# The end of an RWKV-7 layer: other buffers for the raw token sums, the last third of those sums made in two steps, and weight splits placed behind the last root

## The chip, the cores and the metric

The kernel runs on one core of a Trainium2 chip. The metric is the device time of one launch in microseconds (us), as the median of several runs; lower is better. Engines are named as in the profile: PE is TensorE, DVE is VectorE, ACT is ScalarE, POOL is GpSimd, and SP is the engine whose queue issues most of the DMAs. POOL's queue issues the DMAs that add to what lies in memory.

## The reference

Two residual layers work on x of 512 tokens by 2048 columns, all in float32. Layer 0 is gated differential attention; the change does not touch it. Layer 1 is gated RWKV-7 time mixing:

```
p = h @ w_in                                   # h = rms_norm(x)
p = p + (token_shift(p) - p) * mu
r, k, v, g, dw, da = split(p)
...
y = wkv7_scan(r, decay, k, v, -kk, kk * a)     # a 64x64 state per head, 32 heads
mean = y.mean(-1);  var = square(y - mean).mean(-1)
y = (y - mean) * rsqrt(var + GN_EPS)           # per head and token
y = y * gn_w + gn_b + sum(r * k * r_k) * v
y = y * silu(g)
x = x + y @ w_out                              # w_out is 2048 x 2048
```

## The kernel before

**Products.** A float32 product is made as three passes on operands split into a rounded high part and the rest (`mm3`, L116 to L122; L119 is the matmul). A block of weights that a DMA has brought (`wraw`, or the tiles `T2`, `TT0` and `TT1`, which the profile prints as T and TT) is split in halves by `split_w` (L88): ACT casts the high part `wh` (L110), DVE subtracts to get the low part `wl` (L111). There are four buffers of each, and a half block feeds six matmuls in turn: `wh` first, `wl` one matmul later.

**The scan.** The 32 heads are worked on as 16 pairs, j = 0 to 15, in chunks of 64 tokens. `scan_pair` (L1890 to L1934) carries one pair's state through eight chunks. Each chunk is a ring over three engines: a matmul (L1898), two ACT copies `rhs` (L1901), a matmul (L1911), two ACT copies `VS` (L1913), a matmul (L1920), two DVE steps that make the next `VS` (L1924), and two POOL copies `SA` (L1906). Between these steps the scheduler puts matmuls of other products. Each operation of a step stands in the fixed order of its engine, so anything that waits ahead of an ACT copy holds up the ring. After the last chunk come the outputs Y (L1944, L1948), the centring `yc` on DVE (L1952 to L1961), and `normal` (L1964): the squares `ysq` on ACT (L1969), their sums `var` on DVE (L1971), and then the reciprocal root by `rsqrt` (L57 to L70), eleven small DVE operations of which the last writes `rsg`. `scale` (L1977) multiplies `yc` by it, and `finish_y` (L1983) transposes the result on PE (L1989). For pair 15 this is the last root of the kernel, and the gated rows that follow are the last two rows of y that the output product needs.

**The output product.** `y @ w_out` is made for two halves of the columns (`one` and `two`) by a scheme with seven products of blocks in place of eight. It needs sums of blocks of weights (`wsums`) and sums of blocks of tokens. `Sums` (L934) makes both in device memory: a copy is a DMA of SP's queue (L954), an addition is an accumulating DMA of POOL's queue (L958). Of the token sums there are four, S1 to S4, in three thirds i = 0, 1, 2; each is 256 KB. With y's row blocks a, b, c and d they are S1 = b + d, S2 = S1 + a, S4 = S2 + c and S3 = a + b. Each call of `step` does the next item of a list. `Forms.load` (L911) brings the thirds of a sum into raw buffers `fraw` by SP's queue (L916), in a ring of six; `Forms.make` splits them: ACT writes the high part (L931) and DVE the low part (L933), both named fS. DVE's part is ordered behind a given instruction; ACT's is placed where the scheduler finds room.

**The order.** `outputs_of` (L1114 to L1160) is the written order of the end: the blocks "12" of both halves, those "11" of `one` and then of `two`, in whose middle `finish(None)` ends the last scan, and then `rest` of both halves. `pace` feeds split rows of y and takes a step of `Sums`. The scheduler may start instructions of later lines earlier where their operands allow it; `issue_after` gives it an order of two instructions and no more. Each engine then works through its own list strictly in order.

**Buffers.** The six raw buffers of `Forms` are two in the tile LT, two in BK and two of four in G1 (L2109 to L2111). `ysq` lives in LT as well, so the LT pair is free only after the last `ysq`.

Of the kernel before, what the change touches and what calls it, by code (L numbers as in the profile page):

```python
# [13 lines left out]
F32 = mybir.dt.float32  # L14
# [4 lines left out]
ALU = mybir.AluOpType  # L19
# [4 lines left out]
P = 128  # L24
# [33 lines left out]
def rsqrt(g, out, v, n, tag):  # L58

    nc = g.nc  # L60
    sh = g.small.tile([P, n], I32, name="rs_i", tag=tag + "i")
    t = g.small.tile([P, n], F32, name="rs_t", tag=tag + "t")
    nc.vector.tensor_single_scalar(sh[:], v.bitcast(I32), 1, ALU.logical_shift_right)
    nc.vector.tensor_scalar(sh[:], sh[:], -1.0, float(0x5F3759DF), ALU.mult, ALU.add)
    y = sh[:].bitcast(F32)
    for i in range(3):
        nc.vector.tensor_mul(t[:], y, y)
        nc.vector.scalar_tensor_tensor(t[:], t[:], -0.5, v, ALU.mult, ALU.mult)
        o = out if i == 2 else y
        nc.vector.scalar_tensor_tensor(o, t[:], 1.5, y, ALU.add, ALU.mult)  # L70


def load_w(g, raw, block, k0, ks, queue=None):
# [18 lines left out]
@urgent  # L92
def split_w(g, block, kg, cols, k0, raw=None):


    nc = g.nc
    held = raw is not None and block is not None
    if raw is None:
        raw = g.wraw.tile([P, kg, cols], F32, name="wraw", tag="wraw")
        load_w(g, raw, block, k0, slice(0, kg))  # L100
    n = kg // 2
    his, los = [], []
    for k in range(0, kg, n):
        hi = g.wh.tile([P, n, cols], F32R, name="wh", tag="wh")
        lo = g.wl.tile([P, n, cols], F32R, name="wl", tag="wl")
        with ExitStack() as after:
            if held and k0 + k < 4:
                for ins in g.made[k0 + k - 1] if k0 + k else [g.made_prm]:
                    after.enter_context(g.tc.issue_after(ins))
            nc.scalar.copy(hi[:], raw[:, k : k + n])  # L110
            g.split = nc.vector.tensor_sub(lo[:], raw[:, k : k + n], hi[:].bitcast(F32)).ins  # L111
        his.append(hi)
        los.append(lo)
    return Halves(his, n), Halves(los, n)
# [369 lines left out]
class Feed:  # L484
# [8 lines left out]
    def load(self, upto):  # L493
        for k in range(len(self.raw), min(upto, self.n)):
            self.raw.append(self.home(k))
            self.g.nc.sync.dma_start(out=self.raw[k], in_=self.src[k * P : (k + 1) * P, :])
# [257 lines left out]
NS = 6  # L754
KG = 2
# [147 lines left out]
class Forms:  # L903
# [4 lines left out]
        self.at = {nm: [None] * len(homes) for nm in FORMS}  # L908
        self.raw = {}

    def load(self, nm):  # L911
        self.raw[nm] = []
        for i in range(len(self.homes)):
            self.ring.append(self.ring.pop(0))
            raw = self.ring[-1]
            self.g.nc.sync.dma_start(out=raw, in_=self.src[FORMS.index(nm), i])  # L916
            self.raw[nm].append(raw)
# [22 lines left out]
class Sums:  # L940
# [27 lines left out]
    def token_sums(self, i):  # L968
        (a, b), (c, d) = [[self.yd[(FIRST[kb] + i * KG) * P : (FIRST[kb] + (i + 1) * KG) * P,
                                   256 * t : 256 * t + 256].rearrange("(k p) t -> p k t", p=P) for t in range(2)]  # L970
                          for kb in range(2)]
        s1, s2, s3, s4 = [self.forms[n, i] for n in range(4)]
        return [lambda: (self.copy(s1, b), self.copy(s3, a)), lambda: (self.add(s1, d), self.add(s3, b)),
                lambda: self.copy(s2, s1), lambda: self.add(s2, a), lambda: self.copy(s4, s2),
                lambda: self.add(s4, c)]
# [140 lines left out]
def outputs_of(g, one, two, feed, finish, more):  # L1116


    def pace(n):
        feed(4 + n // 2, g.m)  # L1120
        g.wsums.step()

    def then(nm):
        forms.make(nm)
        if nm in order:
            forms.load(order[nm])

    forms, order = one.sums, {"S2": "S4", "S4": "S3"}
    N, s = NS // KG, 0
    for i in range(N + 1):  # L1130
        for b in (one, two):
            pace(s)
            if i == N - 1 and b is two:
                b.want("11")
            b.first12(i)
            s += KG
    two.take("11", two.y)
    for i in range(N):
        pace(s)
        pace(s + 1)  # L1140
        one.first11(i)
        s += KG
        if not i:
            more(0)
            one.want("11")
            one.take("11", one.y)
    one.take("11", one.X, ALU.subtract)
    forms.load("S1")
    for i in range(N):
        two.first11(i)  # L1150
        if i == 0:
            forms.load("S2")
        if i == 1:
            finish(None)
            more(1)
    two.take("11", two.X, ALU.subtract)
    forms.make("S1", g.m.ins)
    one.rest(then, finish)
    two.rest()

# [325 lines left out]
NG = 4  # L1486
# [73 lines left out]


class Pair:
    done, now, scale = False, False, None


def mus(g, i, j):
# [397 lines left out]
def normal(g, p):  # L1964

    nc, w, yc = g.nc, g.work, p.yc
    NG = 2 * NT
    sq = g.low.tile([P, NG, C], F32, name="ysq", tag="LT", bufs=1)
    nc.scalar.activation(sq[:], yc[:], AF.Square)  # L1969
    var = g.small.tile([P, NG], F32, name="var", tag="var")  # L1970
    nc.vector.reduce_sum(var[:], sq[:], AX.X)  # L1971
    nc.vector.tensor_scalar(var[:], var[:], 1.0 / C, GN_EPS, ALU.mult, ALU.add)
    rs = g.small.tile([P, NG], F32, name="rsg", tag="rsg")
    rsqrt(g, rs[:], var[:], NG, "r8")

    def scale():
        nc.vector.tensor_mul(yc[:], yc[:], rs[:, :, None].to_broadcast([P, NG, C]))  # L1977

    p.scale = scale
    if p.now:  # L1980
        p.scale()
# [12 lines left out]
def layer1(g, aps):  # L1994
    nc, tc = g.nc, g.tc
    with ExitStack() as cx:
# [38 lines left out]
        for j in range(D // P):  # L2035
            p = pairs[j]
            if j:
                others = [(1, lambda p=p: turn_keys(g, p, 0)), (2, lambda p=p: turn_keys(g, p, 4)),
                          (4, lambda p=p: turn_values(g, p))]
                if j > 1:  # L2040
                    others.append((5 if j + 1 < D // P else 3, lambda i=j - 2: finish_y(g, i, pairs[i])))
                gaps = (6, 7) if j == 1 else (7, 8) if j < D // P - 1 else (5, 6)
                chain(g, j - 1, pairs[j - 1], 3 if j > 1 else 22, *gaps, others)
            ar = stage2(g, j, r, p)
            for q in pairs[j - 2 : j - 1] if j > 1 else ():
                q.now = True
                if q.scale:
                    with tc.issue_after(ar.ins):
                        q.scale()
            p.now = j + 2 >= D // P  # L2050

            def behind(m, j=j, p=p):
                if j > 1:
                    pairs[j - 2].chain.finish(g)
                with tc.issue_after(m.ins):
                    gram(g, j, p)
                p.solve = Solve(g, t_solve(g, j, p))
            hooks = [(12 if 0 < j < LAG else 18, behind)]
            if j + 1 == D // P:
                hooks.append((39, lambda m, p=p: [mask_gram(g, p, h, m) for h in range(2)]))  # L2060
            stage_v(g, j, p, proj(2, j, behind=hooks + kept()))
            turns = ()
            if j == 0:
                turns = ((9, lambda m: turn_keys(g, p, 0)), (15, lambda m: turn_keys(g, p, 4)),
                         (27, lambda m: turn_values(g, p)))
            if j + 1 < D // P:
                begin(j + 1, turns or kept())

            def finished(m, i=j - LAG):
                with tc.issue_after(m.ins):  # L2070
                    gated(g, i, pairs[i], held)
                g.ys.extend((held, pairs[i].y))

            if j:
                gps = proj(3, j - 1, behind=[(36, finished)] * (j >= LAG) + kept())
                held = gate(g, j - 1, gps, None)
            if j + 1 < D // P:
                r = receptances(j + 1)
        chain(g, j, p, 3, 4, 5, whole=True)
        gts = [held, gate(g, j, proj(3, j), "E")]  # L2080
        feed = Feed(g, g.yd2, KT - 2, lambda k: w.tile([P, T], F32, name="yr", bufs=1, tag=(
# [24 lines left out]
                 {"S1": one("VS"), "S2": one("VS"), "S4": one("xH", "xL"), "S3": one("y", "y")},  # L2106
                 {"S1": one("th0", "th1"), "S2": one("r", "k"), "S4": one("E", "thg"), "S3": one("yc", "v")})

        raws = [g.low.tile([P, 2, KG, 256], F32, name="fraw", tag=t, bufs=1)[:, i] for t in ("LT", "BK") for i in range(2)]  # L2109
        both = w.tile([P, 4, KG, 256], F32, name="fraw", tag="G1", bufs=2)  # L2110
        raws += [both[:, i] for i in range(4)]  # L2111
        sums = Forms(g, g.wsums.forms, raws, homes)

        def sides(c0, early):
# [37 lines left out]
def body(ctx, tc, nc, aps):  # L2152
    g = Ctx()
    g.nc, g.tc = nc, tc
    g.last, g.first, g.ticks, g.kept, g.stored = None, [], 0, None, 0
    g.chains, g.later, g.soon, g.late, g.state, g.solve = [], [], [], [], None, None
    g.hp = ctx.enter_context(tc.tile_pool(name="hp", bufs=16))
    g.wh = ctx.enter_context(tc.tile_pool(name="whp", bufs=4))
# [48 lines left out]
```

## Time and profile before

| what | value |
|---|---|
| median of 3 runs | 2069.09 us (2068.36 to 2069.86) |
| the profiled execution's own time | 2067.63 us |
| its span, first to last instruction | 2065.9 us |
| mean granted TensorE clock | 0.999 |
| DVE, ACT, POOL busy | 82%, 62%, 21% |

A line of the timeline gives the start of a group of instructions in us of the span, its length, the engine, the line of the kernel, the operation, what it writes and reads (buffer numbers left out) with its shape, the number of instructions, and in brackets the idle time of the engine just before it with the instruction or DMA that ended it. Matmuls overlap, so the pace of PE is read from the distance between starts and not from the lengths. A window's line gives the busy time of each engine in that stretch, the number of its instructions, the granted clock (1.00 is full), the DMA engines' busy share and the GB/s moved. A line of DMA issues gives the KB of one and the us from issue to landing.

### The profile page before, as it was taken

What the parts mean: (1) busy time and instruction counts of PE and PEld (TensorE: products, weight loads), DVE (VectorE), ACT (ScalarE), POOL (GpSimd) and SP (SyncE); (2) the same over time, 40 slices, a digit from 0 to 9 for tenths busy, and PEclk for the clock granted to TensorE, in tenths of its full rate; (3) what the DMA queues carried; (4) which work ended last, traced back from release to release, by engine and by line L of the source; (5) the groups of instructions that cost most, each with busy time, mean ns of one, the idle gap of its engine ahead of it and who ended that gap; (6) DMA issues with size and microseconds to landing.
All of it is one profiled execution on the core that took longest, in us unless ns stands there. A gap on an engine that the chain in (4) does not pass through costs nothing.

```text
span 2065.9 us, 35395 instructions
## 1 busy us (share of the span) xinstructions
PE 2044.4 (99%) x11888; PEld 1682.6 (81%) x11888; DVE 1690.7 (82%) x4417; ACT 1288.6 (62%) x3065; POOL 433.4 (21%) x751
## 2 busy tenths in 40 slices
PE   9999999999999999999999999999999999999999
PEld 8888878888888878888778888888888888876787
DVE  5979788897888976576888888888888898887865
ACT  5667676676767754455666666666666666666543
POOL 0020211202111000101232332233333232342000
PEclk9999999999999999999999999999999999999999
DMA  6387877869778665832234443434445332347663
GB/s 201 115 172 184 163 173 175 177 173 168 176 166 212 182 204 180 201 104 95 96 104 131 131 120 97 127 111 130 110 126 136 99 96 86 108 134 214 204 229 133
DMA packets 113943, 306.95 MB, mean 149 GB/s; under 512 B 13920, under 2 KB 35056, under 8 KB 113472
## 3 DMA queue, kind: packets, MB, share of 16 engines
q1 hardware_dynamic: 71056, 204.15, 30.5%
q0 software_dynamic: 28272, 84.52, 23.3%
q10 hardware_dynamic: 14432, 16.01, 2.2%
q8 instruction: 94, 1.54, 0.3%
q14 instruction: 89, 0.73, 0.1%
HBM read 288.63 MB, written 47.45 MB: 163 GB/s over the span
## 4 chain that ended last, share of the span: by engine, by line
PE 43%; DVE 3%; DMA 2%; ACT 1%; issue 1%; SPq 0%; DVEq 0%; ACTq 0%
PE pp L119 31%; PE pt L119 4%; PE sm L1898 1%; PE gp L1669 1%; PE sm L1920 1%; PE sm L1911 1%; DMA forms<-yd 1%; PE Y L1944 1%; DVE wl L111 1%; PE pt L1729 1%; PE px L1796 0%; PE Y L1948 0%; PE px L1811 0%; DMA yr<-yd 0%; PE pt L1989 0%
## 5 line engine op out<-in xcount | busy, mean ns | idle before, releaser
L119 PE MATMUL pp<-hH,wh 128*128 128x512 f32 x1024 | 416.9, 407 | 0.0
L119 PE MATMUL pp<-hL,wh 128*128 128x512 f32 x1024 | 412.1, 402 | 0.0
L119 PE MATMUL pp<-hH,wl 128*128 128x512 f32 x1024 | 411.9, 402 | 0.0
L110 ACT CAST wh<-wraw 128x512 fp32r<-128x512 f32 (+1 forms) x412 | 254.1, 618 | 211.0 <-PE pp L119 139.7
L111 DVE TENSOR_TENSOR wl<-wraw,wh 128x512 fp32r<-128x512 f32 (+1 forms) x412 | 289.9, 705 | 78.2 <-ACT wh L110 73.6
L119 PE MATMUL pp<-wh,hH 128*128 128x512 f32 x784 | 311.7, 398 | 0.7 <-DVE G L383 0.4
L119 PE MATMUL pp<-wl,hH 128*128 128x512 f32 x784 | 308.5, 393 | 0.0
L119 PE MATMUL pp<-wh,hL 128*128 128x512 f32 x784 | 307.8, 393 | 0.0
L119 PEld LDWEIGHTS pp<-hH,wh 128*128 128x128 f32 x1024 | 192.9, 188 | 38.0 <-issue 1.8
L119 PEld LDWEIGHTS pp<-hH,wl 128*128 128x128 f32 x1024 | 193.2, 189 | 33.2
L119 PEld LDWEIGHTS pp<-hL,wh 128*128 128x128 f32 x1024 | 193.2, 189 | 31.3
L119 PE MATMUL pp<-wh,S 128*128 128x512 f32 x672 | 214.4, 394 | 0.0
L616 ACT CAST wh<-T 128x512 fp32r<-128x512 f32 x224 | 137.2, 620 | 91.5 <-PE pp L119 70.9
L1906 POOL COPY SA<-VS 64x64 f32<-64x64 f32 x224 | 76.1, 340 | 494.6 <-DVE VS L1924 446.2
L119 PEld LDWEIGHTS pp<-wh,hH 128*128 128x128 f32 x784 | 147.7, 188 | 31.0 <-DVE acc L1056 0.7
L119 PEld LDWEIGHTS pp<-wh,hL 128*128 128x128 f32 x784 | 148.0, 189 | 30.0
L119 PEld LDWEIGHTS pp<-wl,hH 128*128 128x128 f32 x784 | 147.8, 188 | 28.7 <-DVE wl L111 0.3
L617 DVE TENSOR_TENSOR wl<-T,wh 128x512 fp32r<-128x512 f32 x224 | 150.6, 685 | 23.3 <-ACT wh L616 22.6
L589 POOL DMA_DIRECT2D T<-in_da_w_in_dram x84 | 72.2, 860 | 385.6 <-DMA wraw<-in_da_w_in_dram 193.9
L1762 DVE SCALAR_TENSOR_TENSOR tmpl<-LT,n,Tm 128x60 f32<-128x60 f32 (+24 forms) x496 | 135.9, 274 | 13.3
L119 PEld LDWEIGHTS pp<-wh,S 128*128 128x128 f32 x672 | 124.8, 188 | 24.5
L119 PE MATMUL pp<-wl,S 128*128 128x512 f32 x336 | 132.1, 393 | 0.0
(374 smaller groups left out, 4100.7 us busy)
## 6 DMA issues: line engine op xcount, KB each, us to landing
wraw<-in_rw_w_in_dram SPq DMA_DIRECT2D x128, 512.0 KB, 3.7
T<-in_da_w_in_dram POOLq DMA_DIRECT2D x84, 512.0 KB, 6.7
wraw<-in_da_w_in_dram SPq DMA_DIRECT2D x64, 512.0 KB, 3.9
T<-in_da_w_in_dram SPq DMA_DIRECT2D x28, 512.0 KB, 4.4
wraw<-in_da_w_out_dram SPq DMA_DIRECT2D x26, 512.0 KB, 4.6
wsums<-in_rw_w_out_dram POOLq DMA_DIRECT2D x24, 512.0 KB, 5.9
wraw<-in_da_w_in_dram POOLq DMA_DIRECT2D x21, 512.0 KB, 6.7
wraw<-in_rw_w_out_dram SPq DMA_DIRECT2D x17, 512.0 KB, 4.0
```

Of the source, the lines that this page charges most:

```text
L110: nc.scalar.copy(hi[:], raw[:, k : k + n])
L111: g.split = nc.vector.tensor_sub(lo[:], raw[:, k : k + n], hi[:].bitcast(F32)).ins
L119: m = nc.tensor.matmul(out, a, b, start=s, stop=e, skip_group_check=skip)
L589: self.g.nc.gpsimd.dma_start(out=raw, in_=src, accum_op=ALU.add)
L616: g.nc.scalar.copy(hi[:], raw[:, k])
L617: g.nc.vector.tensor_sub(lo[:], raw[:, k], hi[:].bitcast(F32))
L1669: m = nc.tensor.matmul(gp[h][:, i * P : (i + 1) * P], BK[r_, c0 + i, :, :], p.AR[r_, c0 + i, :, :], start=True, stop=True)
L1729: nc.tensor.transpose(ps[:, i * P : (i + 1) * P], p.BK[:, c0 + i].rearrange("p s t -> p (s t)"), g.ident[:])
L1762: st = nc.vector.scalar_tensor_tensor(tt, LT[:, i : i + 1, i + 1 :].to_broadcast([P, s, n]), n2[:, i : i + 1], Tm[:, 0:s, i : i + 1].to_br ...
L1898: nc.tensor.matmul(sm[:, 0:P], both(p.G[:, c, 0]), both(VS[:, c]), start=True, stop=True)
L1906: g.kept = nc.gpsimd.tensor_copy(p.SA[r_, c - 1, :], VS[r_, c, h, :]).ins
L1911: nc.tensor.matmul(sm[:, P : P + C], both(g.TT[j % 2][:, c]), rhs[:], start=True, stop=True)
```

## The change

Four things change.

1. The raw buffers of `Forms` are all four of G1 and the two of BK; LT is no longer among them.
2. `pace` takes no step of `Sums` any more. The last third's token sums are two steps instead of six: four copies (S1, S2 and S4 from b, S3 from a) at `g.wsums.step()` after the blocks "12", and seven additions (d to S1, S2 and S4, b to S3, a to S2 and S4, c to S4) at a step after `finish(None)`.
3. `forms.load("S1")` is split. The first two thirds are loaded where the whole was; the last third, and S2 behind it, are loaded after `finish(None)`.
4. `rsqrt` returns its last instruction. For the last pair it is kept as `g.root`, and `split_w` orders each DVE subtraction `wl` behind it once 24 more matmuls have been put down (`g.hold`); the DVE parts of S1 are ordered behind it too.

The code of the list of steps, of the loads and of the order after the change:

```diff
@@ split_w
             nc.scalar.copy(hi[:], raw[:, k : k + n])
+            if g.root and g.ticks >= g.hold:
+                after.enter_context(g.tc.issue_after(g.root))
             g.split = nc.vector.tensor_sub(lo[:], raw[:, k : k + n], hi[:].bitcast(F32)).ins
@@ Forms
-    def load(self, nm):
-        self.raw[nm] = []
-        for i in range(len(self.homes)):
+    def load(self, nm, some=None):
+        if nm not in self.raw:
+            self.raw[nm] = []
+        for i in some or range(len(self.homes)):
@@ Sums.token_sums
+        if i == NS // KG - 1:
+            return [lambda: [self.copy(x, y) for x, y in ((s1, b), (s2, b), (s4, b), (s3, a))],
+                    lambda: [self.add(x, y) for x, y in ((s1, d), (s2, d), (s4, d), (s3, b), (s2, a), (s4, a), (s4, c))]]
         return [lambda: (self.copy(s1, b), self.copy(s3, a)), lambda: (self.add(s1, d), self.add(s3, b)),
@@ outputs_of
     def pace(n):
         feed(4 + n // 2, g.m)
-        g.wsums.step()
...
     two.take("11", two.y)
+    g.wsums.step()
...
-    forms.load("S1")
+    forms.load("S1", range(N - 1))
     for i in range(N):
         two.first11(i)
-        if i == 0:
-            forms.load("S2")
         if i == 1:
             finish(None)
+            g.wsums.step()
             more(1)
+    forms.load("S1", range(N - 1, N))
+    forms.load("S2")
     two.take("11", two.X, ALU.subtract)
-    forms.make("S1", g.m.ins)
+    forms.make("S1", g.root)
@@ normal
-    rsqrt(g, rs[:], var[:], NG, "r8")
+    root = rsqrt(g, rs[:], var[:], NG, "r8")
+    if p.last:
+        g.root, g.hold = root, g.ticks + 24
@@ layer1
-        raws = [g.low.tile([P, 2, KG, 256], F32, name="fraw", tag=t, bufs=1)[:, i] for t in ("LT", "BK") for i in range(2)]
         both = w.tile([P, 4, KG, 256], F32, name="fraw", tag="G1", bufs=2)
-        raws += [both[:, i] for i in range(4)]
+        keyed = g.low.tile([P, 2, KG, 256], F32, name="fraw", tag="BK", bufs=1)
+        raws = [both[:, i] for i in range(4)] + [keyed[:, i] for i in range(2)]
```

How the instructions move. The first place is ACT in the last scan, at the chunk where the profile of before shows the longest wait; `sm`, `rhs` and `VS` are the steps of the scan's ring, `yr` a row of y. Before:

```order
L1901 COPY rhs_21941<-sm_21939 64x64 x2
L931 ACTIVATE fS2_22428<-fraw_21729 128x512
L110 CAST wh_22022<-wraw_22020 128x512
L1913 COPY VS_21430<-sm_21939 64x64 x2
L476 CAST hH_21964<-yr_21741 128x512
```

After:

```order
L1909 COPY rhs_21931<-sm_21929 64x64 x2
L111 CAST wh_22011<-wraw_22009 128x512
L1921 COPY VS_21430<-sm_21929 64x64 x2
L479 CAST hH_21954<-yr_21738 128x512
L111 CAST wh_22015<-wraw_22009 128x512
```

The cast of the last third of S2 no longer stands between the two copies of the ring. Before, casts of S4, S2 and S1 (one each, of different thirds) stood among the scan's chunks and one of S4 behind them; now two of S1, whose raw buffers are loaded before the scan, stand ahead of its first chunk, and one of S2 ahead of its last.

The second place is ACT around the squares of the last root. Before:

```order
L931 ACTIVATE fS4_22503<-fraw_21729 128x512
L110 CAST wh_22258<-wraw_22256 128x512
L1969 ACTIVATE ysq_22198<-yc_22191 128x512
L110 CAST wh_22262<-wraw_22256 128x512
L110 CAST wh_22282<-T2_21730 128x512
L110 CAST wh_22286<-T2_21730 128x512
L931 ACTIVATE fS1_22341<-fraw_21725 128x512
```

After:

```order
L935 ACTIVATE fS2_22425<-fraw_21726 128x512
L111 CAST wh_22250<-wraw_22248 128x512
L935 ACTIVATE fS1_22347<-fraw_21725 128x512
L1977 ACTIVATE ysq_22191<-yc_22184 128x512
L111 CAST wh_22254<-wraw_22248 128x512
L111 CAST wh_22271<-T2_21727 128x512
L935 ACTIVATE fS2_22428<-fraw_21726 128x512
L111 CAST wh_22275<-T2_21727 128x512
```

The casts of the last thirds of S1 (fS1_22347) and S2 (fS2_22428) now stand in the middle of this stretch, the first of them directly ahead of the squares, the second between the two halves of T2's weights.

The third place is DVE at the same root; `rs_i`, `rs_t` and `rsg` are the steps of the root, `acc` an accumulation of finished products. Before:

```order
L67 TENSOR_TENSOR rs_t_22205<-rs_i_22204 128x8
L111 TENSOR_TENSOR wl_22283<-T2_21730,wh_22282 128x512
L68 SCALAR_TENSOR_TENSOR rs_t_22205<-rs_t_22205,var_22200 128x8
L1056 TENSOR_TENSOR acc_22137<-acc_22137,pp_22100 128x512
L70 SCALAR_TENSOR_TENSOR rs_i_22204<-rs_t_22205,rs_i_22204 128x8
L1056 TENSOR_TENSOR acc_22137<-acc_22137,pp_22101 128x512
L67 TENSOR_TENSOR rs_t_22205<-rs_i_22204 128x8
L111 TENSOR_TENSOR wl_22287<-T2_21730,wh_22286 128x512
```

After:

```order
L68 SCALAR_TENSOR_TENSOR rs_t_22198<-rs_t_22198,var_22193 128x8
L70 SCALAR_TENSOR_TENSOR rsg_22196<-rs_t_22198,rs_i_22197 128x8
L114 TENSOR_TENSOR wl_22272<-T2_21727,wh_22271 128x512
L1987 TENSOR_TENSOR yc_22184<-yc_22184,rsg_22196 128x512
L114 TENSOR_TENSOR wl_22276<-T2_21727,wh_22275 128x512
L114 TENSOR_TENSOR wl_22316<-wraw_22313,wh_22315 128x512
```

Both subtractions of T2 now stand behind the root's last step. The two accumulations still stand inside the root. On POOL the seven additions stand behind the very last `SA` copy of the last scan, and on SP the load of the last third of S1 waits for the first of them, that of the last third of S2 for the fifth, which itself follows the landing of the second. PE's order is the same but for one small matmul of the scan that moves by one place.

More of the change, by code (lines that the diff above doesn't have):

```diff
@@ L69, in rsqrt @@
         o = out if i == 2 else y
-        nc.vector.scalar_tensor_tensor(o, t[:], 1.5, y, ALU.add, ALU.mult)
+        root = nc.vector.scalar_tensor_tensor(o, t[:], 1.5, y, ALU.add, ALU.mult)
+    return root.ins
 def load_w(g, raw, block, k0, ks, queue=None):
@@ L1562 @@
 class Pair:
-    done, now, scale = False, False, None
+    done, now, scale, last = False, False, None, False
 def mus(g, i, j):
@@ L2078, in layer1 @@
                 r = receptances(j + 1)
+        p.last = True
         chain(g, j, p, 3, 4, 5, whole=True)
@@ L2154, in body @@
     g.nc, g.tc = nc, tc
-    g.last, g.first, g.ticks, g.kept, g.stored = None, [], 0, None, 0
+    g.last, g.first, g.ticks, g.kept, g.stored, g.root, g.hold = None, [], 0, None, 0, None, None
     g.chains, g.later, g.soon, g.late, g.state, g.solve = [], [], [], [], None, None
```

## The prediction

> **What bounds the kernel now.** The page comes first, then windows of 100 us of the second layer's end (columns: length, busy us of PE, PEld, DVE, ACT and POOL with their counts, granted clock, DMA share, GB/s).
>
> ```profile
> span 2065.9 us, 35395 instructions
> PE 2044.4 (99%) x11888; PEld 1682.6 (81%) x11888; DVE 1690.7 (82%) x4417; ACT 1288.6 (62%) x3065; POOL 433.4 (21%) x751
> ```
>
> ```profile
> 1700.00:1800.00 100.00, 99.73 (x747) 82.01 (x746) 86.32 (x230) 63.37 (x157) 32.30 (x62) 1.00 0.33 96
> 1800.00:1900.00 100.00, 96.37 (x705) 76.51 (x704) 86.40 (x235) 63.62 (x160) 35.11 (x66) 1.00 0.55 165
> 1900.00:2000.00 100.00, 95.39 (x472) 76.32 (x471) 73.29 (x133) 49.04 (x96) 8.79 (x14) 0.98 0.66 207
> ```
>
> PE bounds the kernel; no matmul is taken away, so only PE's holes can be won. The window 1900 to 2000 has the most idle time and a clock below 1.00. PE's timeline shows the holes that this change can reach:
>
> ```profile
> 1896.46 0.44 PE L1911 MATMUL sm<-rhs,TT 128*128 128x64 f32 x2 [0.81 <-ACT rhs L1901]
> ...
> 1905.07 0.49 PE L1920 MATMUL sm<-VS,BKT 128*128 128x128 f32 x2 [2.95 <-ACT VS L1913]
> ...
> 1905.63 0.58 PE L119 MATMUL pt<-wh,hL 128*128 128x512 f32 x1
> 1906.01 0.63 PE L119 MATMUL pp<-wh,hH 128*128 128x512 f32 x1
> 1906.43 0.63 PE L119 MATMUL pp<-wl,hH 128*128 128x512 f32 x1
> ...
> 1908.99 0.44 PE L119 MATMUL pp<-wh,hH 128*128 128x512 f32 x1
> ...
> 1936.44 0.55 PE L1989 MATMUL pt<-ident,yc 128*128 128x128 f32 x3 [0.66 <-DVE yc L1977]
> ...
> 1951.39 0.50 PE L119 MATMUL pt<-wh,fS 128*128 128x512 f32 x1 [0.65 <-ACT fS L931]
> ```
>
> Behind the hole of 2.95 us the starts are 0.42 us apart where 0.23 is PE's pace elsewhere (the two rows 1933.12 and 1934.48 below: six steps in 1.36 us). That lasts from 1905.63 to 1908.99, 3.36 us, of which 1 - 0.23/0.42 = 0.45 is lost, 1.5 us; with the step into it I take 1.6. The reach is 0.81 + 2.95 + 1.6 + 0.66 + 0.65 = 6.7 us, 0.3% of the time.
>
> ACT, and the queues behind it, show why the ring of the scan waited:
>
> ```profile
> 1893.78 0.63 ACT L931 ACTIVATE fS<-fraw 128x512 fp32r<-128x512 f32 x1 [1.11 <-DVE VS L1924]
> ...
> 1903.42 0.63 ACT L931 ACTIVATE fS<-fraw 128x512 fp32r<-128x512 f32 x1 [2.87 <-DMA fraw<-forms]
> ...
> 1904.58 0.44 ACT L1913 COPY VS<-sm 64x64 f32<-64x64 f32 x2
> ```
>
> ```profile
> 1899.85 0.49 SPq L954 DMA_DIRECT2D forms<-forms  x1
> 1900.39 0.57 SPq L916 DMA_DIRECT2D fraw<-forms  x1
> ```
>
> ```profile
> 1891.35 1.03 POOL L958 DMA_DIRECT2D forms<-yd  x1
> ```
>
> Read backwards: the `VS` copy at 1904.58 stood behind the cast fS at 1903.42, this waited for its raw load (1900.39), the load stood in SP's queue behind the copy at 1899.85, and that waited for POOL's addition of 1891.35 to land. The 0.81 is the same with a cast at 1893.78.
>
> **Part by part.** Times stay on the clock of the profile before; what is won in the scan shifts all that follows alike. The durations to be put in:
>
> ```profile
> DMA to landing us min/median/max: 4.5/5.5/8.5
> ```
>
> ```profile
> DMA to landing us min/median/max: 2.5/3.6/8.6
> ```
>
> ```profile
> forms<-yd POOLq DMA_DIRECT2D x1, 256.0 KB, 6.9
> ```
>
> The first is that of all additions of token sums, the second that of all raw loads, the third that of the last addition.
>
> *The scan.* The casts that waited are gone from the ring, so 0.81 + 2.95 + 1.6 = 5.4 us goes. In their place two casts of S1 stand ahead of the ring, the first behind this cast:
>
> ```profile
> 1882.01 0.60 ACT L110 CAST wh<-wraw 128x512 fp32r<-128x512 f32 x1
> ```
>
> ```profile
> 1871.05 4.71 SPq L496 DMA_DIRECT2D yr<-yd  x4
> ```
>
> ```profile
> fraw<-forms SPq DMA_DIRECT2D x2, 256.0 KB, 7.7
> ```
>
> The first cast's turn is at about 1882.5. Its raw load follows the four `yr` loads and two weight loads, so at about 1877.1 at the earliest (1871.05 + 4.71 + 2 x 0.65), and lands between 1880.7 (3.6) and 1884.8 (7.7, the loads of the same stretch before): late by 0 to 2.3 us. PE has buffered weights for part of that; I take 0.5. The scan brings 4.9 us.
>
> *The four copies.* They stand in SP's queue behind this load, where SP next did anything at 1899.85:
>
> ```profile
> 1892.58 0.33 SPq L995 DMA_DIRECT2D T<-in_rw_w_out_dram  x1
> ```
>
> Four issues of 0.65 us end at 1895.5, and nobody needs them before the additions: cost nothing, hidden in SP's idle 7 us. Without this cover the next weight load would be 2.6 us later.
>
> *The later holes.* The hole of 0.65 at 1951.39 waited for the cast of a third of S1 that is now made before the scan: it goes. The hole of 0.66 at 1936.44 waited for the root, which on DVE ran between other work:
>
> ```profile
> 1927.86 0.69 DVE L1971 TENSOR_REDUCE var<-ysq 128x8 f32<-128x512 f32 x1
> 1928.46 0.68 DVE L111 TENSOR_TENSOR wl<-wraw,wh 128x512 fp32r<-128x512 f32 x1
> 1929.06 0.16 DVE L1972 TENSOR_SCALAR var<-var 128x8 f32<-128x8 f32 x1
> 1929.26 0.17 DVE L63 TENSOR_SCALAR rs_i<-var 128x8 int32<-128x8 int32 x1
> ...
> 1930.43 0.68 DVE L1056 TENSOR_TENSOR acc<-acc,pp 128x512 f32<-128x512 f32 x1
> 1931.11 0.68 DVE L1056 TENSOR_TENSOR acc<-acc,pp 128x512 f32<-128x512 f32 x1
> ...
> 1935.49 0.17 DVE L70 SCALAR_TENSOR_TENSOR rsg<-rs_t,rs_i 128x8 f32<-128x8 f32 x1
> ```
>
> Twelve small steps at 0.2 us and two accumulations at 0.6 make 3.6 us: begun at 1929.06 the root would be done at 1932.7 and not at 1935.66. That hole goes too; 1.3 us for both. The price of the gate by itself: T2's first `wl` would be ready at 1933.3, and PE takes it in the first of these rows:
>
> ```profile
> 1933.12 0.39 PE L119 MATMUL pt<-wl,hH 128*128 128x512 f32 x1
> ...
> 1934.48 0.39 PE L119 MATMUL pt<-wl,hH 128*128 128x512 f32 x1
> ```
>
> So 0.2 us, if the squares came at their old time. They do not.
>
> *The new wait on ACT.* Directly ahead of the squares stands the cast of S1's last third, and its raw load waits for an addition that POOL issues only behind this:
>
> ```profile
> 1920.44 0.69 POOL L1906 COPY SA<-VS 64x64 f32<-64x64 f32 x1 [0.16 <-DVE VS L1924]
> ```
>
> ```profile
> 1927.19 0.63 ACT L1969 ACTIVATE ysq<-yc 128x512 f32<-128x512 f32 x1 [0.28 <-DVE yc L1961]
> 1927.73 0.60 ACT L110 CAST wh<-wraw 128x512 fp32r<-128x512 f32 x1
> ```
>
> First addition 1921.2, landed 1926.7 (median 5.5), load issued 1926.8, landed 1930.4 (3.6). Cast 0.54, squares at 1930.9 where they were at 1927.19, `var` at 1931.6, 1.2 us to the root's first step (as 1927.86 to 1929.06), 3.6 us of root: 1936.4. T2's first `wl` is ready at 1937.1, 4.0 us after 1933.12. Queued behind the waiting cast are the squares and two `wh`; behind the gate on DVE, `yc` and all the `wl` of the next blocks.
>
> The second cast, of S2, stands before T2's second `wh`. Its load waits for the fifth addition, and this for the landing of the second: issued 1.1 us after the first, 1922.3, landed 1927.8. The fifth then runs behind two others in POOL's queue and beside the loads that SP let go, so I take 6.9 and not 5.5: 1934.7. Load 3.6: 1938.3. Cast 0.54, `wh` 0.6, `wl` 0.68: 1940.1, where 1934.48 was the time: 5.6 us late, the first 4.0 among them. SP's queue is held at the same loads, with `TT0`, two `acc` and two weight loads behind; TT0, held the longest, is first cast late:
>
> ```profile
> 1924.93 0.33 SPq L995 DMA_DIRECT2D TT<-wsums  x1
> ```
>
> ```profile
> 1941.63 0.60 ACT L110 CAST wh<-TT 128x512 fp32r<-128x512 f32 x1
> ```
>
> Issued at 1927.3 it has 14 us: nothing. Without that cover it would add its own lateness, 2.4.
>
> *The clock.* A hole of 2.95 us cost 1.6 more, so one of 4.0 is taken to cost 1.6 too (0 if it is cut by the matmuls between, 3.2 if the second hole brings another dip). The Trainium skill, page TensorE: Matmul & The Clock Gate, Part 1, has the clock halved after at least one idle window of about 3.4 us that runs freely. By it 2.95 us need not halve the clock, the scan's gain would be 1.6 less and the sum 1.6 more; the measured dip of 3.36 us decides against this.
>
> The sum: -4.9 - 1.3 + 5.6 + 1.6 = +1.0 us. On the profiled run's own 2067.63 that is 2068.6; the median of the runs lies 1.46 above it, so 2070.1. About 0.2%, 4.1 us, is what a measurement of this kernel can tell from no change.
>
> **The rivals.**
>
> *Faster: the transfers are short.* POOL's additions run back to back on DMA engines that SP's held queue leaves emptier. With the least rows, 4.5 and 2.5: S1's raw 1928.3, squares 1928.8, root 1934.3, T2's `wl` 1935.0, 1.9 late; S2's raw 1933.8, `wl` 1935.6, 1.1 late. No dip: -6.2 + 1.9 = -4.3, 2064.8. For it: what competes with them is what SP holds back. Against: the fifth follows two others in one queue that have just been issued. The Trainium skill, DMA: Bandwidth & Descriptors, on the fixed cost, fits a transfer by 2.0 us plus its bytes over 436 GB/s: 2.6 us for 256 KB, an estimate by that page that no row here reaches for an addition. By it the raws come before the squares' old time and the result is 2063.1.
>
> *Slower: the additions hold the end.* Seven accumulating transfers at once, with loads beside them, land like the longest row, 8.5. Then S2's raw is there at 1922.3 + 17.0 + 3.6 = 1942.9, T2's `wl` at 1944.7, 10.2 late: -6.2 + 10.2 + 1.6 = +5.6, 2074.7. It decides as soon as the two additions in the chain take more than 15.5 us together (12.4 in my sum, and 3.1 from +1.0 to 4.1). A slow raw load (8.6 is the longest) adds up to 5 to either. For it: both ends of the chain lie on the path with nothing to hide them. Against: it takes the longest landing of all twice in a row.
>
> *No better scan.* The change does not take the wait out of the scan but moves it to its start, as S1's raws land at 7.7 there: 2.3 us in place of 0.5, so +2.8, 2071.9, or 2073.5 with a dip. It needs the load to be as slow as before although the copy of 1899.85's kind that stood ahead of it has been moved away.
>
> **How the numbers follow.** Forecast, 2070.1: 0.50. It is likeliest since all its durations are middle rows. Short transfers 0.17: every one of four would have to be near its least. Long additions 0.22: there are seven at once. No better scan 0.11, of which 0.03 with the dip lies beyond 4.1 us. So faster 0.17, same 0.50 + 0.08 = 0.58, slower 0.22 + 0.03 = 0.25. The range goes from 2064.5, the first rival with a little to spare, to 2076.0, the second with a load 1.3 us above the median; some 0.1 is left out at either side, for it takes the page's price and the long loads to go beyond.
>
> **What would show it.** Right: in the last scan no hole of PE above 0.6 us and a clock of 1.00; ACT idle some 3 to 4 us ahead of the cast of fS before the squares, released by the DMA fraw; two holes of PE before the transposes, 4.0 and 1.6 us, released by DVE's `wl` L114; starts 0.42 us apart behind them; no hole at the first use of S1. Wrong: ACT not idle there (the raws were in time, the gain is whole), a hole of the scan that stays, or additions over 8 us.

## The result, and the profile after

| kernel | median, us | ratio to before, 95% interval |
|---|---|---|
| before (6 runs) | 2068.9 | |
| changed (6 runs) | 2086.8 | 1.0089 (1.0076 to 1.0102) |

The change costs 17.9 us. The profiled execution of the changed kernel spans 2087.3 us and took 2089.3. A hole is a stretch in which PE stands idle. The windows of the changed kernel show where the time goes, with the columns as before:

```profile
1800.00:1900.00 100.00, 95.73 (x702) 76.04 (x701) 86.64 (x238) 62.67 (x157) 31.65 (x60) 1.00 0.50 149
1900.00:2000.00 100.00, 79.70 (x396) 62.37 (x395) 61.82 (x117) 42.38 (x88) 16.29 (x23) 0.90 0.66 183
```

The window 1900 to 2000 lost 15.7 us of busy PE (79.70 where 95.39 was) and its clock went from 0.98 to 0.90. PE's timeline of the changed kernel, the holes around the root:

```profile
1891.97 0.41 PE L1919 MATMUL sm<-rhs,TT 128*128 128x64 f32 x2 [1.48 <-ACT rhs L1909]
...
1933.02 0.50 PE L122 MATMUL pt<-wh,hH 128*128 128x512 f32 x1 [1.77 <-ACT wh L111]
1933.84 0.50 PE L122 MATMUL pt<-wl,hH 128*128 128x512 f32 x1 [0.31 <-DVE wl L114]
...
1937.68 0.50 PE L122 MATMUL pt<-wl,hH 128*128 128x512 f32 x1 [2.18 <-DVE wl L114]
...
1954.36 0.79 PE L122 MATMUL pt<-wh,hH 128*128 128x512 f32 x1 [15.25 <-ACT wh L111]
...
1956.11 0.63 PE L122 MATMUL pt<-wh,hH 128*128 128x512 f32 x1
1956.53 0.63 PE L122 MATMUL pt<-wl,hH 128*128 128x512 f32 x1
...
1960.37 0.42 PE L122 MATMUL pt<-wh,hL 128*128 128x512 f32 x1
```

The holes of 0.81 and 2.95 in the scan are gone, and so are those of 0.66 and 0.65. In their place stand one of 1.48 at the head of the scan and four of 19.5 together at the root. ACT shows what the longest waited for:

```profile
1931.31 0.63 ACT L935 ACTIVATE fS<-fraw 128x512 fp32r<-128x512 f32 x1 [4.85 <-DMA fraw<-forms]
1931.85 0.61 ACT L1977 ACTIVATE ysq<-yc 128x512 f32<-128x512 f32 x1
...
1953.17 0.63 ACT L935 ACTIVATE fS<-fraw 128x512 fp32r<-128x512 f32 x1 [19.68 <-DMA fraw<-forms]
1953.71 0.60 ACT L111 CAST wh<-T 128x512 fp32r<-128x512 f32 x1
```

The two casts of the last thirds of S1 and S2 wait for their raw loads, with the squares behind the first and T2's second `wh` behind the second. POOL shows why the second load is so late:

```profile
1920.00 0.69 POOL L1914 COPY SA<-VS 64x64 f32<-64x64 f32 x1 [0.16 <-DVE VS L1932]
1920.65 1.14 POOL L962 DMA_DIRECT2D forms<-yd  x1
1929.04 1.07 POOL L962 DMA_DIRECT2D forms<-yd  x1 [7.24 <-DMA TT<-in_rw_w_out_dram]
1936.29 1.03 POOL L962 DMA_DIRECT2D forms<-yd  x1 [6.18 <-issue]
1940.99 1.06 POOL L962 DMA_DIRECT2D forms<-yd  x1 [3.67 <-issue]
1945.78 1.04 POOL L962 DMA_DIRECT2D forms<-yd  x1 [3.72 <-issue]
1950.69 1.06 POOL L962 DMA_DIRECT2D forms<-yd  x1 [3.87 <-issue]
```

```profile
1950.40 0.32 SPq L920 DMA_DIRECT2D fraw<-forms  x1
```

The seven additions start 4.7 to 8.4 us apart although the issue of one takes 1.1 and nothing stands between them. These are the DMA issues of the first and of the fourth, with the time to landing at the end:

```profile
forms<-yd POOLq DMA_DIRECT2D x1, 256.0 KB, 8.0
...
forms<-yd POOLq DMA_DIRECT2D x1, 256.0 KB, 4.5
```

The first landed at 1928.65, and the second started at 1929.04; the fourth landed at 1945.5, and the fifth started at 1945.78. The third and the sixth too started 0.3 to 0.4 us after the landing of the one before. POOL starts one of these additions only when the one before has landed. For the second the profile names a load of TT, which the addition does not read and which landed 0.2 us before the first addition (1922.03 + 6.4); from the third to the sixth it names nothing. Only the seventh has to wait, as it adds to the sum of the sixth. SP's load of S2 waited for the fifth, issued 25 us after the first.

How much each stretch changed is read from one instruction in both traces. The same matmul before the last scan stands in this row of before and in this row of the changed kernel:

```profile
1868.28 0.46 PE L1898 MATMUL sm<-VS,G 128*128 128x128 f32 x2 [0.83 <-DVE VS L1924]
```

```profile
1871.00 0.46 PE L1906 MATMUL sm<-VS,G 128*128 128x128 f32 x2 [0.83 <-DVE VS L1932]
```

Up to here the changed kernel's execution is 2.7 us later, which is no work of the change: the instructions are the same, and single executions of one kernel differ by as much (2067.2 to 2070.6 for before). At the last `SA` copy it is 0.44 earlier (1920.00 against 1920.44), so the scan gained 3.2 us. From there to the end it is 21.8 longer (2087.3 - 1920.00 against 2065.9 - 1920.44). Net 18.6, near the 17.9 of the medians.

### The profile page after: what moved, and what is told of

Same layout as the page of the kernel before. It is cut to its first block, busy times and chain, and to the rows that moved or that the text cites. A ratio compares the mean times of both kernels' runs of the same rounds, so it can differ in the third digit from the quotient of the medians.

```text
span 2087.3 us, 35393 instructions
## 1 busy us (share of the span) xinstructions
PE 2047.1 (98%) x11888; PEld 1683.2 (81%) x11888; DVE 1692.2 (81%) x4417; ACT 1288.2 (62%) x3065; POOL 437.5 (21%) x754
## 4 chain that ended last, share of the span: by engine, by line
PE 44%; DVE 2%; issue 2%; DMA 1%; ACT 1%; POOL 0%; SPq 0%; ACTq 0%; DVEq 0%; POOLq 0%
PE pp L122 30%; PE pt L122 5%; PE sm L1906 1%; PE gp L1677 1%; PE sm L1928 1%; PE sm L1919 1%; PE Y L1952 1%; DMA forms<-yd 1%; PE pt L1737 1%; DMA fraw<-forms 0%; DVE wl L114 0%; PE px L1804 0%; PE px L1819 0%; PE Y L1956 0%; PE pt L1999 0%
```

## The experiments

Theory A: POOL starts an addition only when the one before has landed; the sums of the last third are therefore late, and ACT, in strict order, holds PE at each cast whose sum is not there. Rival B: the transfers are all under way and crowd each other. Rival C: the weight splits behind the root hold PE. The runs are numbered as the expectations name them and told in the order of the argument.

**1. The additions in another order.**

```diff
-  ((s1, d), (s2, d), (s4, d), (s3, b), (s2, a), (s4, a), (s4, c))
+  ((s1, d), (s2, d), (s2, a), (s4, d), (s4, a), (s4, c), (s3, b))   # each issued after the one before
```

> The seven additions in another order: both additions to S2 directly behind the first, so that the load of S2's last third waits for the third addition and not for the fifth; a fixed order on POOL, nothing else changed. Theory A (POOL starts one of these additions only when the one before has landed, and ACT, in order, waits for the sum): two landings of 4.4 to 4.9 us fewer, so the hole of 15 us shrinks by about 9.5 and the time is about 2077. Rival B (the additions are all under way and slow each other and the loads): the same bytes are under way, less than 3 us, 2084 to 2087. Rival C (the weight splits ordered behind the root hold PE, not the casts): no change, 2086 to 2087.

Measured 2082.5, ratio 1.0071 (1.0057 to 1.0086). PE's holes in that run:

```profile
1932.18 0.51 PE L122 MATMUL pt<-wl,hH 128*128 128x512 f32 x1 [2.19 <-DVE wl L114]
1939.33 0.79 PE L122 MATMUL pt<-wh,hH 128*128 128x512 f32 x1 [5.72 <-ACT wh L111]
...
1962.12 0.49 PE L122 MATMUL pt<-wh,fS 128*128 128x512 f32 x1 [1.86 <-ACT wh L111]
...
1970.92 0.50 PE L122 MATMUL pt<-wh,hH 128*128 128x512 f32 x1 [2.49 <-DVE acc L1065]
```

The hole of 15.25 became 5.72, the 9.5 that theory A said. The time fell by 4.3, less than half as much, which A had not said: the sums of S4 and S3, now last in line, came too late in their turn. 1.86 and 2.49 us were lost there, and behind the second hole PE ran at half pace for some 3.3 us more (starts 0.43 us apart up to 1975.14).

**2 and 3. The casts behind the last row; and both.**

```diff
+  with ExitStack() as late:                       # last third of S1 and S2 only
+      if nm in ("S1", "S2") and i == len(self.homes) - 1:
+          late.enter_context(self.g.tc.issue_after(self.g.rowhi))   # ACT's split of the last row
       nc.scalar.activation(hi, v, AF.Copy, scale=sign)
```

> The ACT casts of the last thirds of S1 and S2 are ordered behind the split of the last row of y; the additions stay as in the changed kernel. Theory A: the holes of PE of 1.8, 2.2 and 15 us go, the scan keeps its gain of about 3; but SP's queue still waits at the load of S2's last third until the fifth addition has landed (about 1950 of the span) with weight loads behind it, so a later hole of some 5 to 9 us takes the place: 2070 to 2076. Rival B: as A, since the landings stay as they are. Rival C: the gate still holds the weights, over 2080.

Measured 2085.0, ratio 1.0082 (1.0069 to 1.0096): a miss.

> Both together: additions in the order of the first run, casts placed as in the second. Theory A: ACT waits for nothing, SP's queue is free again by about 1941, before the weights behind it are needed: what is left is the gain in the scan (3) and the two small holes (1), so 2064 to 2066 and faster than before. Rival B: crowded transfers keep SP's queue until about 1950, 2070 or more. Rival C: over 2080.

Measured 2084.3, ratio 1.0077 (1.0061 to 1.0092): a miss too. The holes at the root are gone in both, so the casts did hold PE there. But ACT in run 2 now stands further on:

```profile
1950.48 0.63 ACT L938 ACTIVATE fS<-fraw 128x512 fp32r<-128x512 f32 x1 [13.47 <-DMA fraw<-forms]
1951.02 0.60 ACT L111 CAST wh<-TT 128x512 fp32r<-128x512 f32 x1
1959.19 0.63 ACT L938 ACTIVATE fS<-fraw 128x512 fp32r<-128x512 f32 x1 [7.57 <-DMA fraw<-forms]
1959.73 0.60 ACT L111 CAST wh<-TT 128x512 fp32r<-128x512 f32 x1
```

First at S2's cast, then at the first of S4, each with a `wh` of TT behind it. S2's last third is late as a sum: its load waits for the fifth addition. S4's first third is not; its load stands in SP's queue behind that of S2:

```profile
1947.75 0.32 SPq L920 DMA_DIRECT2D fraw<-forms  x1
...
1950.07 0.37 SPq L920 DMA_DIRECT2D fraw<-forms  x1
```

It then took 9.1 us to land, one of eight transfers that SP issued within 3.5 us. PE lost 18.4 us in one hole up to 1962 there (run 3: 8.3, 1.9 and 3.5). The expectation of run 2 had SP's held queue as the next wait, but not the cast of S2 on ACT ahead of it. In run 3 SP's queue was free at about the time expected, but the load of S4 that it issued at 1940.82 took 9.5 us. So the sums of the last third are late, and the loads held back by them come late and all at once; what each of the two costs was not tried apart. Moving one cast moves the hole.

**4. No gate.** The two lines of `split_w` that order `wl` behind the root are left out.

> The changed kernel without the order of the weight splits behind the root. Theory A: the splits wait for ACT's casts anyway, so 2085 to 2088. Rival C: the holes before the transposes go, 2070 to 2080.

One run, 2085.4, inside what theory A gave, with a hole of 16.9 us at the same `wh`. Rival C falls.

**5 and 6. Plain copies; half additions.** `accum_op` left out; and `self.add(x[:64], y[:64])`. Run 5 leaves out the adding in the last third's sums, run 6 one half of their rows.

> The changed kernel with the seven additions made as plain copies by POOL's queue, of the same shape (the sums of the last third are left out: each holds only what was copied last). It asks why POOL starts one only when the one before has landed. If the cause is the accumulation itself, the copies start about 1.1 us apart (the length of an issue) up to the first that waits for another's landing, S2's load comes some 15 us earlier and the time is 2068 to 2072. If the cause is the room for the pieces of such a transfer (256 rows of 1 KB), they still start 4.5 us or more apart and the time stays near 2084.

> The changed kernel with each of the seven additions cut to half of its rows, 128 KB (the other half of the last third's sums is left out). If the room for pieces is the cause, two of them fit and every second one starts directly behind its forerunner, 1.1 us apart. If the accumulation is the cause, each still starts only when the one before has landed, some 3 to 4 us apart. The time is 2070 to 2078 either way.

One run each: 2073.5, above the 2068 to 2072 of the one cause and far below the 2084 of the other, and 2069.6, just below the range. POOL in run 5 and in run 6:

```profile
1921.01 2.10 POOL L962 DMA_DIRECT2D forms<-yd  x3
1926.57 0.66 POOL L962 DMA_DIRECT2D forms<-yd  x1 [3.46 <-issue]
```

```profile
1919.67 2.91 POOL L962 DMA_DIRECT2D forms<-yd  x3
1925.69 0.93 POOL L962 DMA_DIRECT2D forms<-yd  x1 [3.11 <-issue]
```

In both, three start back to back and the fourth is held 3.1 to 3.5 us by something that no semaphore shows. It starts 0.3 to 0.4 us after the first of the three has landed (run 5: 1921.01 + 5.2 = 1926.2; run 6: 1919.67 + 5.7 = 1925.4). So the hold is neither the addition alone (plain copies are held too) nor a rule of one at a time (halves are not): there is a limit on what POOL's queue has under way, which one whole addition, or three halves, or three plain copies fill. Neither expectation had three. What it counts was not found.

**10. All additions in halves.** `for h in (0, 64)` over the same seven, so that nothing is left out.

> The changed kernel with each of the seven additions issued as two of 128 KB; the same sums from the same bytes (the cast of S2's last third also moves three casts later on ACT). If what spaces the additions is the room for the pieces of one transfer, up to three halves are under way at once as in the sixth run, the tenth half is issued near 1938 of the span and not the fifth whole at 1946, and the hole of 15 us shrinks to 4 to 9: 2073 to 2080. If each addition simply takes its time on the DMA engines, halves gain nothing: 2084 to 2090.

Median 2077.2, ratio 1.0032 (1.0022 to 1.0041), inside the expected range and well below the change itself. The same bytes in finer transfers cost less, where rival B counts the bytes alone; and the rows above show the additions one at a time and not all under way. For the additions rival B falls. How much of the gain is theirs stays open, as S2's cast also stands three casts later in this run.

**7 and 8. The old sums beside the scan, the casts late.** In run 7 the old steps of the sums and the old loads, with the change's buffers and gate; every ACT cast of `Forms` is ordered behind `g.rowhi`. In run 8 only that order, in the kernel before.

> The token sums made step by step during the scan, as before the change; of the change stay the other raw buffers and the weight splits behind the root; and all ACT casts of token sums are ordered behind the split of the last row of y. Theory A (what held PE before and after is ACT standing, in order, at a cast whose sum is not there, and the additions must run beside the scan): no cast in the scan and none at the root, so the holes of 0.81, 2.95, 0.66 and 0.65 and the slow clock behind the second go, 6.7 us less 0 to 2 for casts that now stand close together: 2062 to 2065 where before has 2068.5. Rival (the casts bunched behind the last row hold the weights of the products there): 2066 to 2070.

Measured 2065.8, ratio 0.9992 (0.9983 to 1.0001): less than expected, about no change. In the scan of run 7 PE has a hole of 2.72, and DVE and POOL show its cause:

```profile
1906.64 0.60 DVE L1928 SCALAR_TENSOR_TENSOR VS<-sm,gam,Sg 64x64 f32<-64x64 f32 x2 [3.41 <-POOL Sg L1913]
```

```profile
1904.98 1.11 POOL L962 DMA_DIRECT2D forms<-yd  x1 [3.89 <-DMA forms<-forms]
1906.17 0.44 POOL L1913 TENSOR_SCALAR Sg<-SA,gam 128x64 f32<-128x64 f32 x1
```

POOL stood at the last addition, which waits for a copy, with the scan's `Sg` behind it. The kernel before had the same addition in the same place, covered by the hole that ACT's cast made:

```profile
1903.38 1.11 POOL L958 DMA_DIRECT2D forms<-yd  x1 [3.13 <-DMA forms<-forms]
```

The 2.95 had two causes, and taking one away left 2.72.

> The kernel before with nothing changed but the ACT casts of token sums, all ordered behind the split of the last row; buffers, sums and weight splits as before. Theory A: the scan's holes go (0.81, 2.95 and the clock's 1.6), the two later ones stay or grow a little, since the third of S1 in the late buffer still comes late: 2063 to 2066. Rival: the scan needs the additions beside it to be out of the way, not the casts: 2068.

Measured 2073.6, ratio 1.0026 (1.0017 to 1.0035): slower. The scan's hole is 2.71, and 5.28 us are lost at the first use of S1, where ACT's cast waits 3.89 us for its raw load. LT is among the buffers here, as in the kernel before; that it makes this load late is argued and not shown.

**9. The additions one by one in the scan.** As run 7, with four early copies and single additions: two ahead of the scan, then one behind each `Sg`.

> As the seventh run (other raw buffers, weight splits behind the root, all casts of token sums behind the last row's split), and the last third's sums made from four early copies and seven single additions: two ahead of the last scan, then one behind each Sg of it, so that POOL never stands ahead of the scan's next step with an addition that waits for a copy, and never with two. Theory A: the 2.72 us that the seventh run still had in the scan (POOL waiting at an addition for its copy, Sg behind it) go as well, with the slow clock behind them: 2062 to 2065 where before has 2067.5 to 2068.5. Rival (POOL cannot start one addition until the one before has landed, 4.4 to 8.5 us, and a chunk is only about 5 us): POOL holds the scan, holes of 1 to 3 us per chunk, 2068 to 2078.

Measured 2068.9, ratio 0.9998 (0.9989 to 1.0007): the rival came. POOL, in the second half of the scan:

```profile
1908.42 1.11 POOL L962 DMA_DIRECT2D forms<-yd  x1 [5.58 <-DMA forms<-yd]
1909.03 1.05 POOL L1918 COPY SA<-VS 64x64 f32<-64x64 f32 x2
...
1913.38 1.12 POOL L962 DMA_DIRECT2D forms<-yd  x1 [2.77 <-DMA forms<-yd]
...
1919.21 1.11 POOL L962 DMA_DIRECT2D forms<-yd  x1 [3.61 <-issue]
```

POOL stands at each of them. In the first two rows of additions it waits by a semaphore for the addition before, to whose sum this one adds; the third needs no such wait and is held as in the changed kernel. PE's holes there are 2.82, 0.60 and 1.22.

**11 and 12. The gate alone; the buffers alone**, each in the kernel before.

> The kernel before with only the weight splits (and S1's low parts) ordered behind the last root. The root runs without gaps, so the hole of 0.66 before the transposes goes, and at most 0.2 comes at T2's first weights; the scan keeps its holes of 0.81 and 2.95: 2067 to 2069.

One run, 2071.4, above the range. The hole before the transposes is gone as expected; that in the scan was 4.25 in this execution, and 1.72 stood at the first use of S1.

> The kernel before with only the raw buffers exchanged (four of G1 and two of BK). The hole of 0.65 at the first use of S1 goes; two casts of S1 move to the head of the scan, and one cast of S2 stays between the scan's copies, so the hole of 2.95 stays: 2067 to 2070.

One run, 2068.4. The hole at the first use of S1 is gone; in the scan one of 4.19 at its first chunk replaced the 2.95, which had been expected to stay. The list of raw buffers before has eight entries (two of LT, two of BK and all four of G1, L2109 to L2111), not six; the exchange leaves six. No run here tries the number of buffers by itself.

**13. Run 7 with its last addition behind the scan.**

```diff
     def pace(n):
         feed(4 + n // 2, g.m)
-        g.wsums.step()
+        if len(g.wsums.tokens) > 1:
+            g.wsums.step()
...
             finish(None)
+            g.wsums.step()
```

> As the seventh run (sums made step by step beside the scan as before the change, other raw buffers, weight splits behind the root, casts of token sums behind the last row's split), with one addition moved: the last of the third third (c to S4), which waits for a copy, stands behind the last SA of the scan instead of among its steps. Theory A: of the gain in the scan that the sum counted, the seventh run lost 2.72 us and the slow clock behind it to POOL standing at this addition with Sg behind it; S4 is needed last, so the addition costs nothing at its new place: the scan has no hole over 0.4 us, and the time is 4 to 6 us less than before, 2062 to 2065 where before has 2067.5 to 2069.5. Rival (the additions as such, by their landings, slow the scan's POOL steps as in the ninth run): holes of 1 to 3 us stay, within 2 us of before.

Measured 2063.1 (6 runs) beside 2069.6 for before, ratio 0.9969 (0.9956 to 0.9981): 6.5 us faster than before and the best of all. Its windows, and its only holes of PE of 0.3 us or more between 1880 and 1945:

```profile
1800.00:1900.00 100.00, 97.03 (x708) 76.97 (x707) 86.38 (x234) 63.95 (x161) 36.37 (x66) 1.00 0.56 164
1900.00:2000.00 100.00, 98.80 (x492) 79.14 (x492) 76.15 (x137) 50.88 (x98) 7.55 (x12) 1.00 0.70 226
```

```profile
1898.16 0.46 PE L1904 MATMUL sm<-VS,G 128*128 128x128 f32 x2 [0.31 <-DVE VS L1930]
...
1913.06 0.51 PE L122 MATMUL pp<-wh,hH 128*128 128x512 f32 x1 [0.36 <-DVE acc L1060]
```

## Why the prediction was wrong

2070.1 was forecast, 1.0 us slower and too little to tell from no change. 2086.8 was measured, 17.9 slower and outside the range of 2064.5 to 2076.0.

**The step that failed** is the start of the additions: "issued 1.1 us after the first, 1922.3". The length of an issue was taken for the distance of two issues. The second addition started 8.4 us after the first, and the fifth, which was to run at 1927.8, at 1945.78; so S2's raw was not there at 1938.3 but its cast ran at 1953.17. The trace of before had the row that decides this, and the prediction did not use it. These are POOL's rows where two additions of an earlier third stand back to back:

```profile
1645.41 1.12 POOL L958 DMA_DIRECT2D forms<-yd  x1 [0.27 <-DMA forms<-yd]
1650.45 1.07 POOL L958 DMA_DIRECT2D forms<-yd  x1 [3.93 <-issue]
```

They are 5.04 us apart, with 3.93 idle "issue" between; the first took 4.7 to land. As an estimate, with 5.0 per addition in place of 1.1 the fifth would have started at 1941.2, and S2's cast at 1941.2 + 6.9 + 3.6 = 1951.7: 19.0 late in place of 5.6, which makes +14.4 and 2083.5.

**The slower rival** named the right place, the additions ahead of S2's load, but another mechanism: two landings of 8.5 in a row, with the rest beside them. In fact five additions stood one behind the other, with landings of 8.0, 6.9, 4.4, 4.5 and 4.6 us. Its price, 2074.7, and its chance carried the same error as the sum.

**The first wait** was right: 4.0 us forecast up to T2's first `wl`, 1.77 + 0.31 + 2.18 = 4.3 measured, with ACT idle 4.85 us ahead of the cast before the squares (3 to 4 forecast). The closeness is in part luck: the first addition took 8.0 us and not 5.5, the raw load behind it 2.6 and not 3.6.

**The scan** gained 3.2 and not 4.9. The wait at S1's first cast was 1.35 on ACT and 1.48 on PE, and the trace is 2.2 us later there by the same matmuls; the third rival's 2.3 is what happened, not the 0.5 taken. That the holes of 0.81 and 2.95 go was right, but the reason given for the 2.95 was half of it: run 7 shows that POOL's addition was a second cause. The change removed both, by taking the additions out of the scan too; run 13 removes both and keeps the sums in time.

**The later holes** went as forecast, 1.3 us. **The four copies** on SP and **the gate** cost nothing that can be seen: run 4 without the gate is as slow.

**The clock** was mis-sized: half pace lasted from 1954.36 to 1960.37, 6.0 us of which 0.45 is lost, 2.7 and not 1.6.

The terms as measured: -3.2 - 1.3 + 19.5 + 2.7 = +17.7, where the traces differ by 18.6 and the medians by 17.9; some 0.9 us of the trace is not assigned.

**The faster rival** was far off: the raw loads took 2.8 us at 1950.40, near the 2.5 it wanted, but the additions took 4.4 to 8.0. The Trainium skill, DMA: Bandwidth & Descriptors, Anatomy of one DMA, gives 2.6 us for 256 KB, an estimate by that page's fit for DMAs that GpSimd issues; the additions of this case do not follow it. The raw load of SP's queue, which that fit is not for, lies near it.

## What to carry to other kernels

Ask of a queue not how long an issue takes but how far apart two issues stand where nothing is between them, and look for that pair anywhere in the trace: here it stood 270 us earlier. Before an instruction that waits for a transfer is moved, count what stands in order behind it on its own engine; a wait on ACT or POOL that another wait covered is a second cause, and removing the first alone may show no clear gain (run 7). Work that is late as a whole is not helped by moving the one who waits (runs 2 and 3): only the item that need not be early (the last addition, run 13) should go behind the critical stretch.

## What the runs showed of the hardware

Accumulating DMAs of 256 KB (256 rows of 1 KB) from POOL's queue ran one at a time, 4.4 to 8.0 us each, the next 0.3 to 0.4 us after the landing of the one before, and held POOL itself in that time, which the profile puts down as "issue"; three of 128 KB, or three plain ones of 256 KB, were under way at once.

After a hole of 2.95 us PE ran at half pace for 3.4 us, after one of 15.25 for 6.0. The length of the hole alone does not decide: after 2.72 us in run 7 the granted clock was 0.61 from 1907 to 1911, after 2.82 us in run 9 it was 1.00 from 1910 to 1915. The Trainium skill, TensorE: Matmul & The Clock Gate, Part 1, has the full clock back after about one busy window of 3.4 us; the first stretch agrees, the second is longer.
